# Raw weights of the MLP's second product requested on ScalarE's queue, and the transposes of four tiles put later in TensorE's order

## The chip, the cores and the metric

The kernel runs on one core of a Trainium2 chip. The metric is the device time of one execution in microseconds (us). The median of three runs of the kernel before is 2425.84 us (2425.81 to 2425.9); lower is better.

Engines are named as the profile names them: PE (TensorE, matmuls), DVE (VectorE), ACT (ScalarE), POOL (GpSimd) and SP (SyncE, which in this kernel issues nearly all data transfers). "SPq" in a row of the profile is a transfer being issued from SP's queue.

## The reference

Two layers of a decoder over 1024 positions of width 1024, all float32. In each layer a token mixer (a chunked gated MLP in layer 1, differential attention in layer 2) is followed by the part that the change touches, a dense MLP with a squared ReLU:

```python
def _sqrelu_mlp(x, w_up, w_down):
    return jnp.square(jax.nn.relu(x @ w_up)) @ w_down      # 1024 -> 4096 -> 1024

for i in range(DEPTH):                                     # DEPTH = 2
    h = h + _rmsnorm(mixer(_rmsnorm(h, g_mix_pre[i])), g_mix_post[i])
    f = _sqrelu_mlp(_rmsnorm(h, g_ffn_pre[i]), f_w_up[i], f_w_down[i])
    h = h + _rmsnorm(f, g_ffn_post[i])
    gate = jax.nn.sigmoid(_rmsnorm(h, g_ple_pre[i]) @ ple_w_gate[i] + ple_b_gate[i])
    h = h + _rmsnorm(gate * (p[i] @ ple_w_proj[i]), g_ple_post[i])
```

## The kernel before, in words

**Products of float32.** Every factor is cut in two: a high part that PE takes at full rate (ACT copies it, L516 in the MLP), and the rest (DVE subtracts, L517). A product is then three matmuls (`mm3`, L345, L346, L347), each of 128 by 512 outputs.

**The MLP (`ffn`).** The first product is done in 16 blocks of 256 hidden columns by a scheme of seven products in place of eight; its banks are emptied by DVE (L589) and ACT (L604), squared by ACT (L592, L593), and the hidden values are stored to DRAM (`hid`, L597). The second product runs over `steps`, pairs (g, c): g = 0, 1, 2 with 16 steps c each, and g = 3 with 8. A step is 24 matmuls into the banks of four row tiles p, two halves each. Between two values of g the banks are emptied by `evict(g, p)`: g = 0 by ACT L764 and DVE L765, g = 1 by DVE L767 and L768, g = 2 by DVE L770 to L772.

**What a step needs.** `load_down(n)` requests, seven steps ahead: the raw weights (g = 0 and 1: L708, 512 KB into the first buffer of a pair x, and L709, 256 KB into the second; g = 2: L705, two halves of 256 KB), a combination of weights that an earlier g stored (g = 2: L706), and half of a hidden block (L710, 512 KB, straight into the room where PE reads it). `split_down(n)`, two or three steps ahead, combines the raw weights on DVE (L720 and L721, L725 and L726, L731 and L732), stores a combination for later (L727, L733), and cuts hidden block and weights into one of seven rooms. The first buffers of the pairs come from rings: for g = 1 six (hin, hin, xn, xn, raw, bbc), for g = 2 four (raw, hin, hin, bbc). A buffer is free for the next load when DVE's L517 has cut it.

**The end of g = 2.** For the tiles 0 to 3 the second product is complete there. `whole` finishes the post-norm, loads the residual (L329), adds (DVE L333), stores it, and normalises for the next part: squares on ACT (L321), a root on POOL (L243, L244), a scaled copy on ACT (L323). Then `transpose_to` transposes the tile in two halves on PE (L296, four transposes of 128 by 128 each, into one of two banks `pt` in turn), and each half is cut by ACT (L282) and DVE (L283). The second argument of `whole` says when: `defer` puts the transposes off until PE's order has advanced by that many microseconds of an internal count, 0.417 ns a column (`tick`). `US_F` is 11; so tile p's transposes come 13 + 4p counted us after the place of the call.

**What sets the order.** PE's instructions run in the order in which the code is written. The order on the other engines and queues is made by a scheduler that weighs the whole program, so an edit can move instructions that it does not name. An engine runs its order strictly one after the other; a transfer that is issued on an engine's queue and has to wait makes that engine wait. A transfer also waits until an earlier one that shares its completion counter has landed; the program has eight such counters, which the transfers of SP and ACT take in turn.

Of the kernel before, what the change touches and what calls it, by code (L numbers as in the profile page):

```python
# [43 lines left out]
def f32(ap):  # L44
    return ap.bitcast(F32)


def f32r(ap):
    return ap.bitcast(F32R)
# [82 lines left out]
def _trunk(ctx, tc, nc, a, out):  # L132
# [107 lines left out]
    def rstd_of(ss, n, eps):  # L240

        k = ss.shape[1]
        nc.gpsimd.tensor_scalar(out=ss, in0=ss, scalar1=1.0 / n, scalar2=eps, op0=ALU.mult, op1=ALU.add)  # L243
        nc.gpsimd.tensor_tensor(out=ss, in0=ss, in1=mhalf[:, :k], op=ALU.pow)  # L244
# [7 lines left out]
    US_G, US_P, US_F, US_E, US_L, US_T = 3.0, 10.0, 11.0, 14.0, 11.0, 20.0  # L252
# [73 lines left out]
    def residual(tt, t_ap, rs, hsrc, hdst, pre, gain=None):  # L326

        h = hinR.next()
        nc.sync.dma_start(h, hsrc[tt * P:(tt + 1) * P, :])  # L329
        w = D if pre or tt < NT - 1 else 512  # L330
        for c in range(0, D, w):
            cs = slice(c, c + w)
            nc.vector.scalar_tensor_tensor(out=h[:, cs], in0=t_ap[:, cs], scalar=rs, in1=h[:, cs],  # L333
                                           op0=ALU.mult, op1=ALU.add)
            nc.sync.dma_start(hdst[tt * P:(tt + 1) * P, cs], h[:, cs])
        if pre:
            pre_norm(h, tt, pre, gain)
# [3 lines left out]
    def load_gbc(i):  # L341
        nc.sync.dma_start(gbc, a["g_post"][i:i + 1, :].broadcast_to([P, D]))

    def mm3(ps, lh, ll, rh, rl, start, stop):
        nc.tensor.matmul(ps, lhsT=lh, rhs=rh, start=start, stop=False)  # L345
        nc.tensor.matmul(ps, lhsT=lh, rhs=rl, start=False, stop=False)  # L346
        nc.tensor.matmul(ps, lhsT=ll, rhs=rh, start=False, stop=stop)  # L347
        tick(3 * 512)
# [152 lines left out]
    def resident(i, k):  # L501

        hi, lo = f32r(aux(2 * k)), f32r(aux(2 * k + 1))
        nc.sync.dma_start(f32(lo), pD[i][k])
        split(nc, f32(lo), hi, lo, eng=nc.gpsimd)
        return hi, lo

    def ffn(i, hsrc, hdst, next_weights):
# [10 lines left out]
        down = dn.rearrange("(q r p) (c d) -> q r c p d", r=2, p=P, c=2)  # L519
        down_rows = dn.rearrange("(q r p) d -> q r p d", r=2, p=P)  # L520
# [159 lines left out]
        def cols(x, k):  # L680
            return x[:, k * 512:k * 512 + 512]
# [10 lines left out]
        def load_down(n):  # L692
            g, c = steps[n]
            room = last[c] if g == 3 else rooms[n % 7]
            hi, lo = [f32r(x.rearrange("p k t -> p (k t)")) for x in room]
            wh, hh, wl, hl = hi[:, 0:1024], hi[:, 1024:], lo[:, 0:1024], lo[:, 1024:]
            x = sets[g].next() if g < 3 else None
            if g == 3:
                for k in range(2):
                    nc.sync.dma_start(f32(cols(hl, k)), hid[2 * c + k][:, 3072:])  # L700
                nc.sync.dma_start(f32(wl), t4[c])
            else:
                if g == 2:
                    for k in range(2):
                        nc.sync.dma_start(cols(x[0], k), down[c, k, 1])  # L705
                    nc.sync.dma_start(x[1], cols(t4[c // 2], c % 2))  # L706
                else:
                    nc.sync.dma_start(x[0], down_rows[c, 0])  # L708
                    nc.sync.dma_start(x[1], down[c, 1, 1 - g])  # L709
                nc.sync.dma_start(f32(hl), hid[c][:, g * 1024:g * 1024 + 1024])  # L710
            loaded[n] = wh, wl, hh, hl, x

# [30 lines left out]
        def after(t):  # L743

            for n in range(len(steps)):
                if n - t == lead_s[n]:
                    split_down(n)
            for n in range(len(steps)):
                if n - t == lead_l[n]:
                    load_down(n)  # L750
# [8 lines left out]
        def evict(g, p):  # L759
            m11, m12 = cols(MA[:, p], 0), cols(MA[:, p], 1)  # L760
            m21, m22 = cols(MA[:, p + 4], 0), cols(MA[:, p + 4], 1)
            a_, b_ = PM[p], other[p]
            if g == 0:
                act(m11, a_, AF.Copy)  # L764
                vec(out=m21, in0=b_, in1=m11, op=add)  # L765
            elif g == 1:
                vec(out=m11, in0=a_, in1=m11, op=add)  # L767
                vec(out=m12, in0=b_, in1=m21, op=add)  # L768
            elif g == 2:
                vec(out=m22, in0=a_, in1=m12, op=add)  # L770
                vec(out=m12, in0=b_, in1=m12, op=add)
                vec(out=m21, in0=a_, in1=m21, op=add)  # L772
            else:
                vec(out=m21, in0=a_, in1=m21, op=add)

        def half(tt, cb):
            m = cols(MA[:, tt], cb)
            ssq[tt] = small2[:, tt, :]
            act(xnR.next()[:, 0:512], m, AF.Square, accum_out=ssq[tt][:, cb:cb + 1])
            vec(out=m, in0=m, in1=cols(gbc, cb), op=ALU.mult)  # L780

        def whole(tt, us):
            s = ssq[tt]
            vec(out=s[:, 0:1], in0=s[:, 0:1], in1=s[:, 1:2], op=add)
            rstd_of(s[:, 0:1], D, RMS_EPS)
            residual(tt, MA[:, tt, :], s[:, 0:1], hsrc, hdst, us)

        for m, (g, c) in enumerate(steps):
            wh, wl, hh, hl = cuts.pop(m)
            n_c = NQ if g < 3 else NQ // 2  # L790

            for p in range(4):
                for e in range(2):
                    bank = PM[p] if e == 0 or g == 3 else other[p]
                    cw = slice(e * 512, e * 512 + 512)
                    ch = slice(e * 512 + p * P, e * 512 + p * P + P)
                    mm3(bank, hh[:, ch], hl[:, ch], wh[:, cw], wl[:, cw],
                        c == 0 and (g < 3 or e == 0), c == n_c - 1 and (g < 3 or e == 1))
                if c == n_c - 1:
                    evict(g, p)  # L800
                    if g == 3:
                        half(p + 4, 0)
                        whole(p + 4, US_F + 4.0 * p)
            if g == 1 and c == 4:
                load_gbc(2 + i)
            if g == 2 and 2 <= c < 6:
                half(c - 2, 0)
            if c == n_c - 1 and g == 2:
                for p in range(4):
                    half(p, 1)  # L810
                    whole(p, US_F + 2 + 4.0 * p)
                for p in range(4):
                    half(p + 4, 1)
                next_weights(i)
            after(m)
            if g == 3:
                if c < 4:
                    ws.load()
                elif c < 6:
                    res[i] += [resident(i, 2 * c - 8), resident(i, 2 * c - 7)]  # L820
# [476 lines left out]
    with tc.manual_schedule(engines={mybir.EngineType.PE}):  # L1297
        x = a["x"]
# [30 lines left out]
        def gates(i):  # L1329
# [3 lines left out]
            ws.stop = len(ws.specs)  # L1333

        ffn(0, hD[0], hD[1], gates)
        ple(0, hD[1], hD[2], US_E)
        mixer1(1, hD[2], hD[3])
        ffn(1, hD[3], hD[4], gates)
        ple(1, hD[4], out, 0)

# [72 lines left out]
```

## Time and profile before

| | |
|---|---|
| median of 3 runs | 2425.84 us |
| profiled execution | 2432.34 us, of which the span (first to last instruction) is 2430.6 |
| PE busy | 2338.2 us, 96% of the span |
| DVE, ACT, POOL busy | 1609.4, 1151.7, 235.4 us |
| granted clock of PE, mean | 0.981 of full speed |
| moved by transfers | 441 MB, 181 GB/s on average |

Stages of the MLP in layer 2, by the windows of the trace: g = 0 fills about 1980 to 2058 us (transfer engines busy 0.91 of the time, 324 GB/s, ACT busy for 35.12 of the 78 us), g = 1 about 2062 to 2150 (2058 to 2150: 0.71, 233 GB/s, ACT 31.79 of 92), g = 2 from 2162 to about 2270.

How to read it: PE is busy nearly always, so the time that can be won or lost lies where PE waits, and the list of waits says for whom. A row of the timeline has the start in us, the length, the engine, the line of the kernel, the operation, what it writes and reads with its shape, and in brackets how long the engine stood idle before it and who released it.

### The profile page before, as it was taken

How to read it: one execution, taken by the hardware profiler on the slowest of the kernel's cores; microseconds unless marked ns; L12 is line 12 of the kernel's file. 1: busy time of each engine (PE TensorE's matmuls, PEld its weight loads, DVE VectorE, ACT ScalarE, POOL GpSimd, SP SyncE). 2: the span in 40 equal slices, each digit the busy share in tenths (PEclk: the TensorE clock that was granted, in tenths of full speed). 3: DMA queues.
4: the chain of work that ended last, by engine and by line, in shares of the span. 5: the costliest groups of instructions: out<-in, count | busy, mean ns of one | idle time of the engine just before them, and what ended most of it. 6: DMA issues, size and time to landing. Idle time of an engine off the chain costs nothing. (4 is left out here: it accounts for less than half of the span.)

```text
span 2430.6 us, 30336 instructions
## 1 busy us (share of the span) xinstructions
PE 2338.2 (96%) x10748; PEld 1933.6 (80%) x10748; DVE 1609.4 (66%) x2468; ACT 1151.7 (47%) x1929; POOL 235.4 (10%) x303
## 2 busy tenths in 40 slices
PE   9999999999999899999999989998999999979998
PEld 7888878888778677878887878777888888868787
DVE  4742698777865665563344888778877797565654
ACT  6232555555433345462224766556555554334551
POOL 1100200000000013010001342321000000000310
PEclk9999999999999899999999999999999999989999
DMA  9111445446976765244445765654544598767423
GB/s 335 47 35 53 160 143 189 154 152 216 356 246 222 243 230 174 87 160 151 145 150 184 217 176 143 156 182 136 185 149 164 177 351 275 246 222 246 173 104 121
DMA packets 200424, 441.02 MB, mean 181 GB/s; under 512 B 21040, under 2 KB 55856, under 8 KB 200144
## 3 DMA queue, kind: packets, MB, share of 16 engines
q1 hardware_dynamic: 199840, 437.89, 54.0%
q8 instruction: 85, 1.39, 0.2%
q0 software_dynamic: 432, 1.19, 0.2%
q14 instruction: 67, 0.55, 0.1%
HBM read 310.02 MB, written 133.17 MB: 182 GB/s over the span
## 5 line engine op out<-in xcount | busy, mean ns | idle before, releaser
L357 PE MATMUL pm_a<-w,xh 128*128 128x512 f32 x704 | 223.7, 396 | 1.2 <-ACT w L119 0.9
L357 PEld LDWEIGHTS pm_a<-w,xh 128*128 128x128 f32 x704 | 131.6, 189 | 29.1 <-ACT w L119 2.0
L516 ACT ACTIVATE xh<-xl 128x1024 fp32r<-128x1024 f32 x72 | 75.4, 1055 | 147.4 <-DMA xl<-hid 129.2
L357 PE MATMUL pb<-w,xh 128*128 128x512 f32 x416 | 135.9, 403 | 5.2 <-DVE gbc L950 2.9
L357 PE MATMUL pm_a<-w,xl 128*128 128x512 f32 x352 | 138.6, 394 | 0.0
L516 ACT ACTIVATE w<-ma 128x512 fp32r<-128x512 f32 x134 | 84.1, 631 | 104.6 <-PE pm_a L346 34.9
L517 DVE TENSOR_TENSOR xl<-xl,xh 128x1024 fp32r<-128x1024 f32 x72 | 87.4, 1220 | 50.7 <-ACT xh L516 50.7
L825 POOL DMA_DIRECT2D bbc<-in_ple_b_gate_dram x2 | 1.3, 627 | 1118.4 <-DVE xl L517 1118.4
L345 PE MATMUL pm_a<-xh,w 128*128 128x512 f32 x272 | 106.7, 392 | 0.0
L346 PE MATMUL pm_a<-xl,w 128*128 128x512 f32 x272 | 106.3, 391 | 0.0
L347 PE MATMUL pm_a<-xh,w 128*128 128x512 f32 x272 | 106.3, 391 | 0.0
L516 ACT ACTIVATE s<-s 128x1024 fp32r<-128x1024 f32 x56 | 58.3, 1054 | 92.3 <-DMA s<-hid 84.5
L243 POOL TENSOR_SCALAR small<-small 128x1 f32<-128x1 f32 x104 | 49.4, 475 | 543.0 <-DVE small L390 319.7
L357 PEld LDWEIGHTS pb<-w,xh 128*128 128x128 f32 x416 | 77.5, 191 | 19.6 <-DVE gbc L950 3.1
L517 DVE TENSOR_TENSOR w<-ma,w 128x512 fp32r<-128x512 f32 x134 | 91.2, 683 | 0.0
L517 DVE TENSOR_TENSOR s<-s 128x1024 fp32r<-128x1024 f32 x56 | 67.7, 1221 | 34.4 <-ACT s L516 33.6
L345 PE MATMUL pb<-xh,w 128*128 128x512 f32 x216 | 84.5, 391 | 0.0
L347 PE MATMUL pb<-xh,w 128*128 128x512 f32 x216 | 84.1, 389 | 0.0
L346 PE MATMUL pb<-xl,w 128*128 128x512 f32 x216 | 84.1, 389 | 0.0
L357 PE MATMUL pb<-w,xl 128*128 128x512 f32 x208 | 83.1, 400 | 0.0
L333 DVE SCALAR_TENSOR_TENSOR hin<-ma,small,hin 128x1024 f32<-128x1024 f32 (+1 forms) x49 | 61.6, 1260 | 28.4 <-POOL small L244 13.9
L357 PEld LDWEIGHTS pm_a<-w,xl 128*128 128x128 f32 x352 | 66.6, 189 | 13.0
(468 smaller groups left out, 7005.5 us busy)
## 6 DMA issues: line engine op xcount, KB each, us to landing
xl<-hid SPq DMA_DIRECT2D x56, 512.0 KB, 4.9
ma<-in_f_w_up_dram SPq DMA_DIRECT2D x48, 512.0 KB, 3.6
h<-hin SPq DMA_DIRECT2D x40, 512.0 KB, 3.3
hid<-ma SPq DMA_DIRECT2D x80, 256.0 KB, 2.4
s<-hid SPq DMA_DIRECT2D x40, 512.0 KB, 5.0
hin<-h SPq DMA_DIRECT2D x40, 512.0 KB, 3.4
hid<-xn SPq DMA_DIRECT2D x64, 256.0 KB, 2.8
hid<-hin SPq DMA_DIRECT2D x64, 256.0 KB, 2.8
```

The lines of the kernel that those rows point to most:

```text
L243: nc.gpsimd.tensor_scalar(out=ss, in0=ss, scalar1=1.0 / n, scalar2=eps, op0=ALU.mult, op1=ALU.add)
L333: nc.vector.scalar_tensor_tensor(out=h[:, cs], in0=t_ap[:, cs], scalar=rs, in1=h[:, cs], op0=ALU.mult, op1=ALU.add)
L345: nc.tensor.matmul(ps, lhsT=lh, rhs=rh, start=start, stop=False)
L346: nc.tensor.matmul(ps, lhsT=lh, rhs=rl, start=False, stop=False)
L347: nc.tensor.matmul(ps, lhsT=ll, rhs=rh, start=False, stop=stop)
L357: nc.tensor.matmul(ps, lhsT=xs(l, kc, tt * P), rhs=r[:, cs], start=kc == 0 and k == 0, stop=kc == KC - 1 and k == 2)
L516: act(h, v, AF.Copy)
L517: vec(out=l, in0=v, in1=f32(h), op=sub)
L825: nc.gpsimd.dma_start(bbc, a["ple_b_gate"][i:i + 1, :].broadcast_to([P, D]))
```

## The change

The raw weights of the second product, L705, L708 and L709, are issued on ACT's queue (`nc.scalar`) in place of SP's: 96 transfers per layer. L706 and L710, the stores and everything of g = 3 stay on SP. And the transposes of the tiles 0 to 3 at the end of g = 2 are put off by 5 counted us more.

```diff
             else:
                 if g == 2:
                     for k in range(2):
-                        nc.sync.dma_start(cols(x[0], k), down[c, k, 1])
+                        nc.scalar.dma_start(cols(x[0], k), down[c, k, 1])
                     nc.sync.dma_start(x[1], cols(t4[c // 2], c % 2))
                 else:
-                    nc.sync.dma_start(x[0], down_rows[c, 0])
-                    nc.sync.dma_start(x[1], down[c, 1, 1 - g])
+                    nc.scalar.dma_start(x[0], down_rows[c, 0])
+                    nc.scalar.dma_start(x[1], down[c, 1, 1 - g])
                 nc.sync.dma_start(f32(hl), hid[c][:, g * 1024:g * 1024 + 1024])
...
             if c == n_c - 1 and g == 2:
                 for p in range(4):
                     half(p, 1)
-                    whole(p, US_F + 2 + 4.0 * p)
+                    whole(p, US_F + 7 + 4.0 * p)
```

Both edits move other instructions, in both layers alike but for details. Three places, all of which name tiles as the profile does (`xl`, `s`: rooms of step data; `raw`, `bbc`, `hin_79`, `hin_80`: raw buffers; `t_1_j`: stored combinations of layer 2).

First, the passage from g = 1 to g = 2 in layer 2. SP before, from the store of the second buffer's combination (hid_15 is the hidden block of the last step of g = 1, hid_0 that of the first step of g = 2):

```order
L733 DMA t_1_0_169<-ma 128x512
L706 DMA ma<-t_1_1_170 128x512
L705 DMA hin_80<-in_f_w_down_dram 128x512
L706 DMA ma<-t_1_2_171 128x512
L710 DMA xl_69<-hid_14_159 128x1024
L733 DMA t_1_1_170<-ma 128x512 x2
L706 DMA ma<-t_1_3_172 128x512 x2
L710 DMA xl_70<-hid_15_160 128x1024
L710 DMA s_71<-hid_0_145 128x1024
L705 DMA raw<-in_f_w_down_dram 128x512 x2
L710 DMA xl_70<-hid_1_146 128x1024
```

SP now, from the same store:

```order
L733 DMA t_1_0_169<-ma 128x512
L706 DMA ma<-t_1_2_171 128x512
L733 DMA t_1_1_170<-ma 128x512
L710 DMA xl_69<-hid_14_159 128x1024
L706 DMA ma<-t_1_3_172 128x512
L733 DMA t_1_1_170<-ma 128x512
L706 DMA ma<-t_1_3_172 128x512
L710 DMA xl_70<-hid_15_160 128x1024
L710 DMA s_71<-hid_0_145 128x1024
L710 DMA xl_70<-hid_1_146 128x1024
```

The raw loads are gone, hid_14 stands behind the first of the two stores to t_1_1, hid_15 still behind both, and hid_1 directly behind hid_0. ACT, the same place (steps 32 to 36, + is what is new there):

```order
 L516 ACTIVATE s_71<-raw 128x1024
+L705 DMA raw<-in_f_w_down_dram 128x512
 L516 ACTIVATE s_71<-s_71 128x1024
+L705 DMA raw<-in_f_w_down_dram 128x512
 L516 ACTIVATE xh_68<-hin_79 128x1024
 L516 ACTIVATE xh_68<-xl_70 128x1024
+L705 DMA hin_79<-in_f_w_down_dram 128x512 x2
 L516 ACTIVATE s_73<-hin_80 128x1024
 L516 ACTIVATE s_73<-s_73 128x1024
+L705 DMA hin_80<-in_f_w_down_dram 128x512 x2
 L516 ACTIVATE xh_67<-bbc 128x1024
```

Behind the last row the two halves for bbc stand again with a cut of a hidden half (`xh_67<-xl_69`) between them.

Second, ACT at the end of the first product (layer 1; `gbc` here is a hidden value on its way out, `s_72<-s_72` the cut of a hidden half):

```order
 L516 ACTIVATE xh_68<-ma 128x1024
 L592 ACTIVATE gbc<-gbc 128x512
+L708 DMA raw<-in_f_w_down_dram 128x1024
+L593 ACTIVATE gbc<-gbc 128x512
 L516 ACTIVATE s_72<-s_72 128x1024
-L593 ACTIVATE gbc<-gbc 128x512
 L516 ACTIVATE s_71<-ma 128x1024
+L708 DMA ma<-in_f_w_down_dram 128x1024
+L709 DMA ma<-in_f_w_down_dram 128x512
 L516 ACTIVATE xh_68<-ma 128x1024
```

Raw loads stand among the cuts there, and L593 ahead of a cut that it followed.

Third, the transposes at the end of g = 2 in layer 2. PE now, from the first transposes (24 matmuls later than before) on; the next transposes, of tile 1, come 18 matmuls and one group of transposes behind the first row:

```order
L296 MATMUL pt_88<-identr,ma 128x128 x4
L345 MATMUL pm_c_11160<-xh_68 128x512
L346 MATMUL pm_c_11160<-xl_70,xh_68 128x512
L347 MATMUL pm_c_11160<-xh_68,xl_70 128x512
L296 MATMUL pt_89<-identr,ma 128x128 x4
L345 MATMUL pm_c_11161<-xh_68 128x512
```

ACT at that place, before and now (the two L323 are tiles 0 and 1, the first two L321 tiles 2 and 3):

```order
 L323 ACTIVATE ma<-hin_79,small 128x1024
 L323 ACTIVATE ma<-hin_80,small 128x1024
+L321 ACTIVATE ma,small<-hin_79 128x1024
+L321 ACTIVATE ma,small<-hin_80 128x1024
+L113 ACTIVATE s_72<-s_72 128x1024
 L282 ACTIVATE xh_67<-pt_88 128x4x128
-L282 ACTIVATE xh_67<-pt_89 128x4x128
-L321 ACTIVATE ma,small<-hin_79 128x1024
-L282 ACTIVATE xh_67<-pt_88 128x4x128
-L113 ACTIVATE s_72<-s_72 128x1024
-L321 ACTIVATE ma,small<-hin_80 128x1024
 L323 ACTIVATE ma<-hin_79,small 128x1024
```

L282 of tile 0's first half stood directly behind the two L323; now two L321 and an L113 stand ahead of it.

## The prediction

> **What bounds the kernel now.** I read the page first: TensorE (PE) is busy for 2338.2 of 2430.6 us, so a change can only win or lose time where PE stands still. The list of what each engine waited for, PE's rows, names those places (columns: who waits on whom, us in total, times, longest):
>
> ```profile
> PE pm_c L345 <- DVE ma L767: 12.7, 1, 12.7
> PE pm_a L345 <- DVE ma L767: 9.5, 1, 9.5
> PE pt L296 <- ACT ma L323: 8.8, 2, 4.4
> PE pm_a L345 <- DVE gbc L589: 4.1, 1, 4.1
> PE pb L345 <- DVE ma L765: 3.1, 1, 3.1
> ...
> PE pm_c L345 <- DVE gbc L589: 0.6, 1, 0.6
> ```
>
> The L589 rows are the end of the MLP's first product (layer 1, then layer 2), the others lie in its second. The two L767 waits are one place, once per layer: the passage from g=1 to g=2 (layer 2 has the 12.7). The L323 waits are the first transposes at the end of g=2, once per layer. A stop also costs clock afterwards; the windows around the two places of layer 2, and PE's rows after the long stop, show it:
>
> ```profile
> 2150.00:2180.00 30.00, 16.69 (x57) 13.00 (x57) 24.22 (x31) 13.04 (x18) 0.00 (x0) 0.72 0.66 222
> 2262.00:2300.00 38.00, 33.59 (x153) 27.48 (x152) 22.42 (x28) 24.19 (x39) 16.50 (x14) 0.91 0.64 221
> ```
>
> ```profile
> 2162.75 0.77 PE L345 MATMUL pm_c<-s 128*128 128x512 f32 x1 [12.69 <-DVE ma L767]
> ...
> 2169.43 0.63 PE L346 MATMUL pm_c<-s 128*128 128x512 f32 x1
> 2169.85 0.63 PE L347 MATMUL pm_c<-s 128*128 128x512 f32 x1
> ```
>
> The granted clock is 0.72 and 0.91 there (the number ahead of the last two), and matmuls start 0.42 us apart after the stop, against 0.23 elsewhere (two rows further below). So a stop that vanishes is worth more than its length, but one that only grows costs its growth alone: the slow matmuls behind it are paid already.
>
> **Step one: why PE waits at L767.** Number the steps n = 16g + c, so that 32 is the first of g=2. DVE's rows of layer 2, and SyncE's queue and ScalarE (ACT) beside them:
>
> ```profile
> 2119.84 0.68 DVE L732 TENSOR_TENSOR ma<-ma,hin 128x512 f32<-128x512 f32 x1
> ...
> 2130.77 1.23 DVE L517 TENSOR_TENSOR xl<-xl,xh 128x1024 fp32r<-128x1024 f32 x1 [5.96 <-ACT xh L516]
> 2131.91 1.22 DVE L517 TENSOR_TENSOR s<-raw,s 128x1024 fp32r<-128x1024 f32 x1
> ...
> 2136.71 0.69 DVE L731 TENSOR_TENSOR raw<-raw 128x512 f32<-128x512 f32 x1 [2.44 <-DMA raw<-in_f_w_down_dram]
> ...
> 2144.19 1.22 DVE L517 TENSOR_TENSOR s<-hin,s 128x1024 fp32r<-128x1024 f32 x1
> ...
> 2161.31 0.69 DVE L731 TENSOR_TENSOR raw<-raw 128x512 f32<-128x512 f32 x1 [1.36 <-DMA raw<-in_f_w_down_dram]
> 2161.92 0.68 DVE L767 TENSOR_TENSOR ma<-pm_c,ma 128x512 f32<-128x512 f32 x1
> ```
>
> ```profile
> 2118.07 2.80 SPq L733 DMA_DIRECT2D t<-ma  x2
> 2121.95 1.11 SPq L706 DMA_DIRECT2D ma<-t  x2
> 2123.11 0.42 SPq L710 DMA_DIRECT2D xl<-hid  x1
> ...
> 2133.16 0.81 SPq L705 DMA_DIRECT2D raw<-in_f_w_down_dram  x2
> ...
> 2140.68 0.38 SPq L710 DMA_DIRECT2D s<-hid  x1
> ```
>
> ```profile
> 2129.68 1.06 ACT L516 ACTIVATE xh<-xl 128x1024 fp32r<-128x1024 f32 x1 [6.29 <-DMA xl<-hid]
> ...
> 2145.53 1.06 ACT L516 ACTIVATE s<-s 128x1024 fp32r<-128x1024 f32 x1 [5.33 <-DMA s<-hid]
> ```
>
> The eviction L767 had its input long before (PE stopped at 2162.75 - 12.69 = 2150.06). It stands on DVE behind L731 of step 40, and that L731 ends a loop of five rounds: DVE cuts a raw buffer (L517, over at 2133.13), the buffer is asked for again (L705, 2133.16), lands, is combined (L731, 2136.71), and only then does DVE cut the next buffer. From 2136.71 to 2161.31 it goes round four times, 6.15 us each. The loop's start, 2133.13, hangs on the cut of step 31's hidden half (2130.77, DVE idle for 5.96), on its load's landing (ACT idle for 6.29), and that load was issued at 2123.11, last in SyncE's row behind stores L733 and re-loads L706.
>
> **The change on this place.** In the changed order DVE's rows from L731 of step 36 to L767 are the same but for one swap. A weight load is issued 0.03 us after its buffer comes free now, so SyncE does not hold the loop up and there is nothing for the new queue to shorten. What may shorten is the loop's start. But the order shows step 31's load (hid_15) still behind the same stores L733 and re-loads L706: the last store needs L732 (2119.84), the re-load the end of that store. It therefore goes at about 2123 again; I take no gain. The ends: if it came so early that DVE's 5.96 vanished, -6.0; step 30's load now stands behind a store that it used to precede, and the loads of steps 31 to 33 go out together, so +2.0 (most of the 2.80 us that the two L733 take).
>
> ACT's new order does cost time in the loop, because the raw loads now stand in line with cuts. Steps 36 and 39: the second half's request stands behind the cut of a hidden half, 1.05 us each. Step 38: the pair stands behind the cut at 2145.53, which waits for the load issued at 2140.68 and ends at 2146.59, while DVE frees the buffer at 2144.19 + 1.22 = 2145.41: 1.2 us. Against that the one swap lets DVE cut the bbc buffer ahead of an L732, -0.6. Sum 1.05 + 1.05 + 1.2 - 0.6 = **+2.7 us per layer, +5.4 in all**, with ends of -3.3 and +4.7 per layer. The 96 requests per layer themselves (0.33 us each, as the single SyncE issues) are hidden: ACT is busy for 13.04 of the 30 us of the window above.
>
> A rule speaks against any gain here. The Trainium skill, "DMA: Bandwidth & Descriptors", section "Issuing engines are not separate DMA queues", says that requests from several engines interleave on the same 16 DMA engines, and that a second issuer saves only the sequencer's time of issue. The rows agree as far as they go: the wait is for landing, not for issue. By the rule alone this term would be 0, not +5.4.
>
> **Step two: the start of the second product.** PE's stop at L589 in layer 1:
>
> ```profile
> 608.43 1.06 ACT L516 ACTIVATE s<-s 128x1024 fp32r<-128x1024 f32 x1 [0.74 <-DMA s<-hid]
> 609.40 0.61 ACT L593 ACTIVATE gbc<-gbc 128x512 f32<-128x512 f32 x1
> ```
>
> ```profile
> 609.87 1.22 DVE L517 TENSOR_TENSOR s<-s 128x1024 fp32r<-128x1024 f32 x1
> ...
> 615.68 0.68 DVE L589 TENSOR_TENSOR gbc<-pm_a,hin 128x512 f32<-128x512 f32 x1
> ```
>
> DVE runs without a gap up to this L589, which frees PE's bank. Now ACT has raw loads among its cuts here: a load L708 that must wait for an earlier transfer, the same hidden half that the cut at 608.43 waits for, then L593 (0.61), and only then that cut. So the cut is 0.33 + 0.61 = 0.9 us late. It was ready at 609.49 and DVE took it up at 609.87, so 0.4 of that is hidden and DVE's chain, L589 at its end, is 0.5 late. I take **+0.5 per layer, +1.0 in all**; ends 0 (DVE has other work to put first) and +3 per layer (ACT's next two requests wait for transfers too). In layer 2 the wait is 0.6 today, so nothing hides it there.
>
> The passage g=0 to g=1: in layer 1 the first L765 comes earlier in DVE's order and the last comes behind an L725 that waits for a load. I take 0, and price the bad case as a rival.
>
> **Step three: the transposes.** PE, ACT and DVE rows at the end of g=2, layer 2:
>
> ```profile
> 2269.69 0.39 PE L346 MATMUL pm_c<-s 128*128 128x512 f32 x1
> 2269.92 0.39 PE L347 MATMUL pm_c<-s 128*128 128x512 f32 x1
> 2274.72 1.12 PE L296 MATMUL pt<-identr,ma 128*128 128x128 f32 x4 [4.41 <-ACT ma L323]
> ...
> 2280.33 0.40 PE L345 MATMUL pm_c<-xh 128*128 128x512 f32 x1
> ```
>
> ```profile
> 2273.52 1.15 ACT L323 ACTIVATE ma<-hin,small 128x1024 f32<-128x1024 f32 x1 [4.37 <-POOL small L244]
> ...
> 2280.56 1.06 ACT L321 ACTIVATE ma<-hin 128x1024 f32<-128x1024 f32 x1 [1.95 <-DVE hin L333]
> ...
> 2283.58 1.06 ACT L113 ACTIVATE s<-s 128x1024 fp32r<-128x1024 f32 x1
> ```
>
> ```profile
> 2277.00 0.69 DVE L283 TENSOR_TENSOR xl<-pt,xh 128x512 fp32r<-128x512 f32 x1 [4.72 <-ACT xh L282]
> ...
> 2280.72 1.28 DVE L333 SCALAR_TENSOR_TENSOR hin<-ma,small,hin 128x1024 f32<-128x1024 f32 x1 [0.20 <-DMA hin<-h]
> ```
>
> The first transposes move 24 matmuls down: 24 x 0.23 = 5.5 us, from 2270.15 to 2275.6. L323 ends at 2274.67, so their wait vanishes, with 0.9 us to spare. With the slow work behind it (nine matmuls and two groups of four transposes took 2274.72 to 2280.33, 5.6 us; at 0.23 each, four transposes of 128 columns counted as one matmul of 512, an estimate, they would take 2.5) it is worth 4.4 + 3.1 = 7.5 us per layer.
>
> But ACT's order changes with it. Its cut of tile 0's transposes (L282) stood right behind the two L323; now L321 of tile 2, L321 of tile 3 and L113 stand ahead of it. L321 of tile 3 needs DVE's L333, which starts at 2280.72 on a load of the residual and ends at 2282.00. From there: L321 1.06 and its read 0.18, L113 1.06, L282 0.60, DVE's L283 0.69, about 2285.2 with the small overlaps that such rows have. PE needs the bank back for tile 1's transposes, 18 matmuls and two transpose groups after tile 0's: 2275.6 + 20 x 0.23 = 2280.2. So PE stops there for 5.0 us instead, with the same slow matmuls behind: **+0.6 per layer, +1.2 in all**. The stall goes from L323 to L283; it is not removed. Ends: -7.5 per layer if the cuts come in time, +3 if L333 also comes later by the delays of step one's kind.
>
> **The sum.** 5.4 + 1.0 + 0 + 1.2 = +7.6 us. The profiled execution took 2432.34 us and would take 2439.9; it lies 6.5 us over the median of the runs, so the median goes from 2425.84 to **2433.4**.
>
> **The rivals.**
> - *The transposes' wait really goes* (scheduled rows are late in the order, not in time; ACT is idle for 4.37 ahead of L323, so it has room): -15.0 with the rest as above, 6.4 - 15.0 = -8.6, **2417.2**. Against it: L333 waits for a load that is issued only once L323 frees the buffer.
> - *Both stalls shrink*: with L705 and L709 gone from SyncE, step 31's load no longer comes late, -3.3 per layer, so -6.6 - 15.0 + 1.0 = -20.6, **2405.2**. For it: DVE's 5.96. Against it: the stores L733 stay ahead of that load.
> - *The queue is only a label*: transfers land as before and cuts hide what the order does; only +1.2 is left, **2427.0**. This is what the Trainium skill's rule named above would give.
> - *ACT holds the evictions*: from g=0 to g=1, ACT's L764 and DVE's L765 wait behind a raw load. The price is one landing:
>
> ```profile
> 709.30 0.33 SPq L708 DMA_DIRECT2D bbc<-in_f_w_down_dram  x1
> ```
>
> ```profile
> 714.04 0.69 DVE L725 TENSOR_TENSOR bbc<-bbc 128x512 f32<-128x512 f32 x1 [1.24 <-DMA bbc<-in_f_w_down_dram]
> ```
>
> 4.7 us from issue to use, with L708's issue and L725 5.8, plus 3.1 of slow clock: 8.9 in layer 2, and 8.9 less the 3.1 us of today's wait in layer 1, 14.7 on top of the 7.6, **2448.1**. It decides from the point where that landing comes after the first matmul of g=1 that needs the bank.
>
> **Chances.** The forecast 0.50 (own range 2427 to 2442), the label 0.17, the transposes' gain 0.15, both gains 0.10, the held evictions 0.08. The range 2413 to 2446 leaves out the last two. A measurement of this kernel tells about 0.2%, 4.9 us, from no change; some of the forecast's own range lies within that. Faster 0.25, same 0.20, slower 0.55.
>
> **What would show it.** PE's waits after: L767 at 15.4 (layer 2) and 12.2; no L296 wait on L323, but one of some 5 us per layer on L283; L589 near 4.6 and 1.1. Rounds of L731 between 2133 and 2162 that are 7.2 us long where a cut stands between two L705. I am wrong if step 31's hidden half lands well before DVE's last cut of g=1, if ACT's L282 is ready when PE comes to tile 1, or if PE stops inside g=0.

## The result

The changed kernel takes 2442.76 us (median of 5 runs, 2434.09 to 2443.29), against 2425.9 for the kernel before on the same chip: ratio 1.0055, 95% interval 1.0033 to 1.0076. So it is slower by 16.9 us, with an interval from 8.0 to 18.4. The profiled execution took 2443.29 us with a span of 2441.5. Against the profile shown before it is 10.95 us longer, because that execution lay 6.5 us above its own median. The comparison of places below goes by the two profiles.

PE's waits in the changed kernel (who waits on whom, us in total, times, longest):

```profile
PE pm_c L345 <- DVE ma L767: 17.2, 1, 17.2
PE pm_a L345 <- DVE ma L767: 12.5, 1, 12.5
PE pt L296 <- DVE xl L283: 9.2, 3, 4.6
PE pb L345 <- DVE ma L765: 5.6, 2, 5.2
...
PE pm_a L345 <- DVE gbc L589: 3.5, 1, 3.5
...
PE pm_c L345 <- DVE hin L589: 1.3, 1, 1.3
...
PE pm_a L345 <- DVE hin L589: 1.2, 1, 1.2
...
PE pm_c L345 <- DVE gbc L589: 1.0, 1, 1.0
```

The two long stops at L767 grew from 12.7 to 17.2 us and from 9.5 to 12.5. The stops of the transposes on L323 (8.8 in all) are gone, and stops on L283 stand in their place (4.6 and 4.25; the third, 0.35, lies elsewhere). L765 went from 3.1 to 5.6, L589 has two more rows, on `hin`, and a stop of 0.9 us on ACT's eviction L764 is new. The page's part on DMA queues (packets, bytes, share of the 16 engines' time) shows the move itself:

```profile
q1 hardware_dynamic: 172192, 370.77, 45.1%
q10 hardware_dynamic: 27648, 67.12, 8.4%
```

q10 is ScalarE's queue. The 437.89 MB that were all on q1 before are the same bytes, on two queues.

How much later the changed kernel is, at the first matmul behind a stop (start in us):

| place | before | after | later by |
|---|---|---|---|
| layer 1, behind L589 | 616.50 | 616.47 | 0.0 |
| layer 1, behind L765 | 709.93 | 712.32 | 2.4 |
| layer 1, behind L767 | 807.73 | 813.65 | 5.9 |
| layer 2, behind L589 | 1978.30 | 1984.91 | 6.6 |
| layer 2, behind L767 | 2162.75 | 2176.05 | 13.3 |
| last matmul | 2422.76 | 2433.68 | 10.9 |

Nearly all the loss arises between the end of the first product and L767, in both layers (5.9 and 6.7 us; 0.7 more lies between the two stretches). What comes after L767 in layer 2, the transposes with it, adds nothing; it takes 2.4 us back.

### The profile page after: what moved, and what is told of

Read it like the earlier page. It is cut to its first block, busy times and chain, and to the rows that moved or that the text cites. A ratio compares the mean times of both kernels' runs of the same rounds, so it can differ in the third digit from the quotient of the medians.

```text
span 2441.5 us, 30205 instructions
## 1 busy us (share of the span) xinstructions
PE 2335.0 (96%) x10748; PEld 1929.3 (79%) x10748; DVE 1609.2 (66%) x2468; ACT 1152.0 (47%) x1929; POOL 236.5 (10%) x303
## 4 chain that ended last, share of the span: by engine, by line
PE 69%; DVE 11%; DMA 11%; ACT 4%; issue 3%; POOL 2%; SPq 0%; ACTq 0%; DVEq 0%; POOLq 0%
PE pm_a L357 10%; PE pb L357 6%; PE pm_a L347 5%; PE pm_a L346 5%; PE pm_a L345 5%; PE pb L345 4%; PE pb L346 4%; PE pb L347 4%; PE pm_c L345 4%; PE pm_c L346 4%; PE pm_c L347 4%; PE pm_c L357 3%; DMA xn<-in_f_w_down_dram 1%; DMA raw<-in_f_w_down_dram 1%; DMA t<-ma 1%
## 5 line engine op out<-in xcount | busy, mean ns | idle before, releaser
L516 ACT ACTIVATE xh<-xl 128x1024 fp32r<-128x1024 f32 x72 | 75.4, 1055 | 147.5 <-DMA xl<-hid 82.1
L517 DVE TENSOR_TENSOR xl<-xl,xh 128x1024 fp32r<-128x1024 f32 x72 | 87.4, 1221 | 64.7 <-ACT xh L516 64.6
L516 ACT ACTIVATE w<-ma 128x512 fp32r<-128x512 f32 x134 | 83.8, 630 | 95.7 <-PE pm_a L346 31.4
L516 ACT ACTIVATE s<-s 128x1024 fp32r<-128x1024 f32 x56 | 58.4, 1055 | 103.5 <-DMA s<-hid 48.1
L517 DVE TENSOR_TENSOR w<-ma,w 128x512 fp32r<-128x512 f32 x134 | 91.2, 682 | 0.1
L333 DVE SCALAR_TENSOR_TENSOR hin<-ma,small,hin 128x1024 f32<-128x1024 f32 (+1 forms) x49 | 61.7, 1260 | 42.7 <-DMA hin<-h 27.2
L517 DVE TENSOR_TENSOR s<-s 128x1024 fp32r<-128x1024 f32 x56 | 67.8, 1221 | 32.3 <-ACT s L516 32.2
L357 PEld LDWEIGHTS pm_a<-w,xl 128*128 128x128 f32 x352 | 66.9, 190 | 13.3
```

Source lines behind the costliest of these rows:

```text
L357: nc.tensor.matmul(ps, lhsT=xs(l, kc, tt * P), rhs=r[:, cs], start=kc == 0 and k == 0, stop=kc == KC - 1 and k == 2)
L516: act(h, v, AF.Copy)
L517: vec(out=l, in0=v, in1=f32(h), op=sub)
```

## Experiments

Times are medians; each ratio, with its 95% interval, is to runs of the kernel before on the same chip (medians of 2426.0 to 2427.3 us).

**The two halves of the change.** Alone, the transposes put off by five counted microseconds more:

```diff
-                    whole(p, US_F + 2 + 4.0 * p)
+                    whole(p, US_F + 7 + 4.0 * p)
```

> Only the transposes are put later (by 5 counted us); all raw loads stay on SyncE's queue. My theory: ScalarE's order at the end of g=2 comes from this edit alone, so PE's wait of 4.4 us on L323 turns into one of some 4.6 us per layer on L283 (the changed kernel has 4.59 and 4.25), with the same slow matmuls behind it; L767 stays at 9.5 and 12.7, and the time stays within 3 us of the kernel before. Rival: the order on ScalarE does no harm by itself, both waits vanish, and the time falls by about 15 us to some 2411.

2425.99 us, ratio 0.9997 (0.9981 to 1.0013): no change. And the raw loads alone on ScalarE's queue (the three `nc.scalar` lines of the change):

> Only the queue of the raw loads is changed; the transposes stay where they were. My theory: all of the loss is here, so the time is that of the changed kernel within 3 us (about 11 us over the kernel before, profiled); L767 near 12.5 and 17.2, L765 near 5 in layer 1, L323 back at 4.4 twice and no wait on L283. Rival: the two edits only lose together, and this one alone stays within 3 us of the kernel before.

2437.21 us, ratio 1.0049 (1.0032 to 1.0066). The loss is all in the queue. PE's waits, first of the transposes alone, then of the queue alone:

```profile
PE pm_c L345 <- DVE ma L767: 12.6, 1, 12.6
PE pm_a L345 <- DVE ma L767: 9.8, 1, 9.8
PE pt L296 <- DVE xl L283: 9.3, 3, 4.5
```

```profile
PE pm_c L345 <- DVE ma L767: 15.4, 1, 15.4
PE pm_a L345 <- DVE ma L767: 11.4, 1, 11.4
PE pt L296 <- ACT ma L323: 9.2, 3, 4.4
PE pb L345 <- DVE ma L765: 5.7, 2, 4.9
```

With the transposes alone the wait only changes its name, 8.8 us on L323 to 9.3 on L283 (0.5 of them elsewhere). With the queue alone L767 and L765 grow too, L767 somewhat less than in the whole change. The two halves add up to 10.8 us, inside the interval of the whole change.

**Which loads.** Only the 256 KB halves of g = 2 (L705) moved:

```diff
-                        nc.sync.dma_start(cols(x[0], k), down[c, k, 1])
+                        nc.scalar.dma_start(cols(x[0], k), down[c, k, 1])
```

> Only L705 (the raw halves of g=2) is issued on ScalarE's queue; L708 and L709 stay on SyncE's; transposes as before. My theory: the rounds between step 36's and step 40's L731 are hardly longer (in the changed kernel the second half's request went out as the cut ahead of it started, not when it ended), so L767 grows by about 1 us per layer and the time by 1 to 3 us. Rival, as the prediction had it: the rounds cost 2.7 us per layer, 5.4 in all.

2431.68 us, ratio 1.0028 (1.0014 to 1.0042). Only the loads of g = 0 and 1 (L708, L709) moved:

```diff
-                    nc.sync.dma_start(x[0], down_rows[c, 0])
-                    nc.sync.dma_start(x[1], down[c, 1, 1 - g])
+                    nc.scalar.dma_start(x[0], down_rows[c, 0])
+                    nc.scalar.dma_start(x[1], down[c, 1, 1 - g])
```

> Only L708 and L709 (g=0 and g=1) are issued on ScalarE's queue; L705 stays on SyncE's; transposes as before. My theory: most of the loss is here, 8 to 10 us: L708 into bbc stands behind the eviction L764 that waits for TensorE (2.4 us of load loop lost per layer, felt at L767), and L765 of layer 1 near 5. Rival: if L705 is the cause, the time is within 3 us of the kernel before.

2438.0 us, ratio 1.0054 (1.0039 to 1.007): about all of the loss, though the prediction had put most of it into L705. The profiled execution of this kernel was the shortest of its ten runs (2429.78) and shows no longer L767 (12.0 and 8.9), only L765 of layer 1 at 5.1; that of the kernel with L705 moved (2429.16, also below its median) shows neither (L767 at 11.7 and 9.5, L765 at 2.9). So where these two kernels lose their time the traces don't show. The two losses add up to 17.7 us (12.9 to 27 by their intervals) against 11.0 (7.8 to 16.0) for both moved together; the intervals overlap, so whether they simply add stays open.

**Another engine's queue.** The same three loads with `nc.gpsimd` in place of `nc.scalar`; GpSimd has next to no other work there, so nothing stands ahead of a request:

> The raw loads L705, L708 and L709 are issued on GpSimd's queue, which is nearly idle in these stages, in place of ScalarE's; transposes as before. My theory: the loss comes from raw loads standing in one order with ScalarE's cuts and evictions, not from a second queue, so here L767 and L765 stay near those of the kernel before and the time is within 5 us of it. Rival: two queues whose transfers run at the same time are the cause; then L767 and L765 grow as with ScalarE's queue and the time is 8 us or more over the kernel before. (GpSimd may take longer to issue a transfer, so a loss there alone would not tell the two apart.)

2439.76 us, ratio 1.0059 (1.0039 to 1.0078). The theory that the raw loads lose time behind the cuts in ACT's order had the time near that of before, and finds no support; since GpSimd also takes longer to issue a load (0.54 us against 0.33 for a 256 KB half), this run alone does not refute it. One thing still stood between this and "the queue does it": with each placement the scheduler also puts VectorE's and ScalarE's own instructions into another order.

**Queue and order told apart.** The next three kernels hold VectorE's and ScalarE's computing instructions to a written-out order, by edges that order instructions on one engine and wait for nothing (`_ORDER` lists each engine's instructions). In the traces the rows of VectorE and ScalarE stand in exactly the order of the kernel named, and PE's do too. SyncE's order is not held: of its 1106 other transfers 20 stand in another place than before with the loads on ScalarE's queue, and 132 with the loads on GpSimd's.

```diff
+        _pin(tc, nc, _mybir)
...
+def _pin(tc, nc, mb):
+    traced = {i.name: i for i in nc.cur_bb.bb.instructions}
+    for eng, text in _ORDER.items():
...
+            if prev is not None:
+                tc.add_manual_dep(i, prev.name, mb.DependencyInfo(mb.DependencyClass.NoSync, ...))
+            prev = i
```

Loads on ScalarE's queue, order of the kernel before:

> The raw loads are requested on ScalarE's queue, but VectorE's and ScalarE's computing instructions are held to the order that they have in the kernel before (edges of order alone, no waits). With the raw loads moved, the scheduler had given both engines another order. Theory A, the loss comes from that other order of the cuts and subtractions: within 3 us of before, L767 waits near 11.7 and 9.5 us, L765 near 3. Theory B, the loss comes from the queue itself (requests behind ACTIVATEs in ScalarE's order, transfers of two queues side by side): 8 to 11 us slower, L767 near 15 and 11.5, landings of the 512 KB ma loads 7.3 us against 7.0.

2439.91 us, ratio 1.0049 (1.0029 to 1.0068). Loads on SyncE's queue, order of the kernel with moved loads:

> The other half: every load stays on SyncE's queue, but VectorE's and ScalarE's computing instructions are held to the order that they have when the raw loads are on ScalarE's queue. Theory A (the order): 8 to 11 us slower than before, L767 near 15 and 11.5, L765 near 5 in layer 1, L589 above 3 us and a second stop on hin. Theory B (the queue): within 3 us of before, L767 near 11.7 and 9.5.

2432.44 us, ratio 1.0017 (1.0007 to 1.0028). Loads on GpSimd's queue, order of the kernel before:

> The raw loads on GpSimd's queue, which has next to nothing else to do there, VectorE's and ScalarE's computing instructions held to the order of before. With its own order this queue cost 13.7 us. Theory A (the order): within 3 us of before. Theory B (two queues at once; the landings on this queue were 0.4 to 1.0 us longer): 8 to 14 us slower, L767 near 15 and 11.

2463.98 us, ratio 1.0143 (1.0127 to 1.0159). PE's waits, loads on ScalarE's queue in the order of before, then loads on SyncE's queue in the moved order:

```profile
PE pm_c L345 <- DVE ma L767: 17.4, 1, 17.4
PE pm_a L345 <- DVE ma L767: 15.8, 1, 15.8
...
PE pb L345 <- DVE ma L765: 4.4, 2, 3.3
```

```profile
PE pm_c L345 <- DVE ma L767: 12.1, 1, 12.1
PE pm_a L345 <- DVE ma L767: 9.0, 1, 9.0
...
PE pm_a L345 <- DVE gbc L589: 5.5, 1, 5.5
...
PE pb L345 <- DVE ma L765: 2.8, 1, 2.8
```

With the old order the queue costs its full 12.6 us (7.0 to 16.5; L767 at 17.4 and 15.8). The new order by itself costs 5.2 us (interval 1.7 to 6.8) and lengthens only L589 in its trace (8.2 us in all against 4.7, though the kernel with the transposes alone has the same row of 5.5). So the move to another queue is the cause, with the small changes in SyncE's order that come with it. The scheduler's new order, far from causing the loss, softens it on GpSimd's queue (36.7 us in the old order, 13.7 in the new); on ScalarE's the two can't be told apart (12.6 and 11.0).

The traces side with this at L767: in all five kernels with the three loads moved off SyncE's queue its stops are 14.9 to 18.1 us in layer 2 and 11.0 to 18.6 in layer 1. In the five that leave all of them on SyncE's queue and compute the same product, the kernel before among them, they are 10.9 to 12.7 and 8.7 to 9.8.

**Where the queue loses it.** The rows of the requests at the passage g=0 to g=1 of layer 2, and DVE's row that waits for `bbc`. Before:

```profile
2062.78 0.33 SPq L708 DMA_DIRECT2D bbc<-in_f_w_down_dram  x1
...
2065.86 0.33 SPq L710 DMA_DIRECT2D s<-hid  x1
```

```profile
2067.57 0.69 DVE L725 TENSOR_TENSOR bbc<-bbc 128x512 f32<-128x512 f32 x1 [1.29 <-DMA bbc<-in_f_w_down_dram]
```

The raw load L708 is asked for at 2062.78, the hidden half L710 behind it at 2065.86; `bbc` is used at 2067.57, 4.8 us after its request. Changed kernel:

```profile
2071.40 0.38 SPq L710 DMA_DIRECT2D s<-hid  x1
```

```profile
2071.59 0.33 ACTq L708 DMA_DIRECT2D bbc<-in_f_w_down_dram  x1
```

```profile
2078.80 0.69 DVE L725 TENSOR_TENSOR bbc<-bbc 128x512 f32<-128x512 f32 x1 [2.84 <-DMA bbc<-in_f_w_down_dram]
```

Here the hidden half is asked for 0.19 us *ahead* of the raw load, and `bbc` is used 7.2 us after its request. With both on SyncE, the hidden half stood behind raw loads that wait for their buffers (L708, and at 2065.11 an L705). On a queue without them only a store holds it back (L727, at 2070.98), and its 512 KB are under way together with the load that DVE is waiting for: by the trace the two land at 2078.53 and 2078.71. That they slow each other is a reading of these rows. The DMA engines were not full meanwhile (busy 0.71 of the time from 2071.40 to 2078.70, 251 GB/s), so what exactly slows them stays open. The kernel with loads on ScalarE's queue in the old order has both cases in one execution, first with the raw load ahead, then with the hidden half ahead:

```profile
704.32 0.33 ACTq L708 DMA_DIRECT2D raw<-in_f_w_down_dram  x1
...
2070.62 0.33 ACTq L708 DMA_DIRECT2D bbc<-in_f_w_down_dram  x1
```

```profile
705.33 0.38 SPq L710 DMA_DIRECT2D xl<-hid  x1
...
2070.43 0.38 SPq L710 DMA_DIRECT2D s<-hid  x1
```

```profile
708.51 0.69 DVE L725 TENSOR_TENSOR raw<-raw 128x512 f32<-128x512 f32 x1 [1.49 <-DMA raw<-in_f_w_down_dram]
...
2078.25 0.69 DVE L725 TENSOR_TENSOR bbc<-bbc 128x512 f32<-128x512 f32 x1 [3.56 <-DMA bbc<-in_f_w_down_dram]
```

Raw ahead by 1.0 us: 704.32 to 708.51, 4.2 us. Hidden ahead by 0.19: 2070.62 to 2078.25, 7.6 us. The same count for every L708 on which DVE waited (idle for 0.3 us or more; time from the last request for a buffer of that name to DVE's L725. Three times below 2 us are left out, where that request is already the next one; by the request before it they are 6.8 us in the change, 7.0 with the queue alone and 5.1 with L708 and L709 moved):

| kernel | a hidden half asked for less than 1 us ahead | otherwise: count, range, median |
|---|---|---|
| before | none | 15, 4.4 to 6.05, 5.2 |
| only L705 moved | none | 15, 4.5 to 5.9, 5.1 |
| change | 7.2, 7.3 | 14, 3.9 to 7.05, 5.3 |
| queue alone | 6.9, 7.4 | 14, 3.85 to 7.0, 5.1 |
| only L708, L709 moved | 6.0, 8.4 | 11, 4.2 to 6.0, 4.7 |
| ScalarE's queue, old order | 7.6, 7.7, 7.7, 10.2 | 13, 4.2 to 6.0, 5.0 |

Against the median beside it such a load takes 1.3 to 3.7 us longer, mostly 2 to 2.7, and it happens only where L708 is on the other queue. The 10.2 is not one to compare: it is a load requested early (at 604.38, when the first product of layer 1 still runs), and in the kernel before the load at that place took 7.9 us to land.

On ScalarE's and SyncE's queues it matters how close the two requests are, not only which goes first. The long times among the others (6.8 and 7.05 in the change, 6.5 and 7.0 with the queue alone), and the two of 6.8 and 7.0 left out, belong to loads with a hidden half asked for 0.45 to 0.87 us *behind* them: these six landed after 6.4 to 7.0 us. On one queue, six kernels have eight such loads, with the hidden half 0.42 to 0.95 us behind, and they landed after 5.0 to 5.8 us. (With the raw load on GpSimd's queue a hidden half 0.73 to 0.86 us behind did no harm: 4.8 to 5.5 us.) And a meeting alone does not make L767 longer: the trace with only L708 and L709 moved has two (8.4 and 6.0) and an L767 like that before.

L705 lands later too, where a single half is at stake; before and after, in layer 2:

```profile
2108.49 0.33 SPq L705 DMA_DIRECT2D hin<-in_f_w_down_dram  x1
2108.92 0.38 SPq L710 DMA_DIRECT2D s<-hid  x1
```

```profile
2111.03 0.69 DVE L731 TENSOR_TENSOR hin<-hin 128x512 f32<-128x512 f32 x1 [2.56 <-DMA hin<-in_f_w_down_dram]
```

```profile
2118.37 0.38 SPq L710 DMA_DIRECT2D s<-hid  x1
```

```profile
2119.62 0.34 ACTq L705 DMA_DIRECT2D hin<-in_f_w_down_dram  x1
```

```profile
2124.32 0.69 DVE L731 TENSOR_TENSOR hin<-hin 128x512 f32<-128x512 f32 x1
```

2.5 us from request to use before; 4.7 after, with a hidden half asked for 1.25 us ahead. In this order DVE's cut of the half before it stands in between, but the trace has the load landing at 2124.30, just ahead of its use, so it is the landing that came later.

GpSimd's queue loses in another way as well. Its request and DVE's use, in the loop of rounds before L767, old order:

```profile
2162.07 1.06 POOL L705 DMA_DIRECT2D hin<-in_f_w_down_dram  x2 [6.72 <-DVE xl L517]
```

```profile
2167.09 0.69 DVE L731 TENSOR_TENSOR hin<-hin 128x512 f32<-128x512 f32 x1 [4.18 <-DMA hin<-in_f_w_down_dram]
```

Issuing the pair takes 1.06 us in place of 0.81, and DVE uses it 5.0 us after the request, against 3.55 before (2133.16 to 2136.71), so the rounds of L731 are 7.7 to 10 us long where they were 6.15. Meetings with a hidden half cost less there (four in the old order, 5.5 to 6.3 us against a median of 5.1; one in the new, 8.8, beside three with the hidden half 0.04 to 0.16 us behind, 6.5 to 7.4). How its loss divides between the two I did not settle.

**The order of requests on one queue.** Hidden half first, everything on SyncE:

```diff
+                nc.sync.dma_start(f32(hl), hid[c][:, g * 1024:g * 1024 + 1024])
                 if g == 2:
...
-                nc.sync.dma_start(f32(hl), hid[c][:, g * 1024:g * 1024 + 1024])
```

> One queue as before, and the same order on VectorE, ScalarE, GpSimd and TensorE; only the hidden half of a step is requested ahead of the step's raw weights instead of behind them. It is what a second queue does to the bytes in flight: hidden halves no longer stand behind raw weights. If the bytes' order matters (a part of theory B), the raw weights land later and it is 3 to 6 us slower, with longer L767. If not (theory A), within 2 us of before.

2428.19 us, ratio 0.9998 (0.9985 to 1.0011). This run does not test what it was meant to: SyncE's rows show the scheduler putting the hidden half behind the raw load again (L709 here is the L708 of the other kernels, L703 the hidden half):

```profile
2056.82 0.33 SPq L709 DMA_DIRECT2D bbc<-in_f_w_down_dram  x1
...
2059.88 0.33 SPq L703 DMA_DIRECT2D s<-hid  x1
```

So a run that puts the hidden half ahead on *one* queue is missing. That the meeting of the two transfers lengthens the raw load rests on the table above and on the loads with equal spacing on one and on two queues, not on an edit that makes or breaks it alone. How much of the whole loss these meetings make is not shown.

**The transposes with room.** Tile 0 as in the change, tiles 1 to 3 five counted microseconds later still, loads on SyncE's queue:

```diff
-                    whole(p, US_F + 2 + 4.0 * p)
+                    whole(p, US_F + 7 + 4.0 * p + (5 if p else 0))
```

> As the run with only the transposes put later, but the tiles 1 to 3 come 5 counted us later still (24 matmuls more between tile 0 and tile 1). My theory (the stall is ScalarE's L282 standing behind two L321 and an L113, which are ready at about 2285 where PE comes to tile 1 at 2280): PE now comes at 2285.7, no wait on L323 or L283 of more than 1 us is left, and the time falls by 2 x (4.4 + 3.1) = 15 us to some 2411. Rival: L282 falls behind again by as much as PE is late, a wait of 4 to 5 us stays, and the time is within 3 us of the kernel before.

2422.53 us, ratio 0.998 (0.9969 to 0.9991): faster than both kernels.

```profile
PE pt L296 <- DVE xl L283: 3.3, 3, 1.4
...
PE pm_c L345 <- ACT xh L516: 0.8, 1, 0.8
```

The stop is now mostly gone (3.3 us in all on L283, 8.8 on L323 before), but only about 3 us in layer 2 came of it, not the 7.5 that the prediction gave for its going: from the L772 stop to the last matmul the kernel takes 160.0 us in place of 163.0. The stop of 4.4 us became one of 1.4 on L283 and two small ones on cuts of g = 3 (L516 0.8, L517 0.6), 1.6 us less in all; so some 1.4 us were won on the slow matmuls behind it, to which the prediction gave 3.1.

**Two runs that miss their question.** One raw buffer fewer in g = 2 (three of four), and rooms exchanged at the loop's start, were meant to shift that start:

```diff
-            Ring([(x, cols(MA[:, t], 1)) for t, x in zip(range(4, 8), [raw] + hin + [bbc])]),
+            Ring([(x, cols(MA[:, t], 1)) for t, x in zip(range(4, 7), [raw] + hin)]),
```

> The kernel before with three raw buffers for g=2 in place of four (raw, hin, hin). My theory: PE waits at L767 because VectorE's order puts rounds of the load loop ahead of it, as many as the buffers let the scheduler run ahead; with three buffers one round of 6.15 us fewer stands ahead (eight L731 in place of nine), so L767 falls from 12.7 to about 6.5 and from 9.5 to about 3.4, and the time by 12 us to some 2414. Rival: the wait is a shortage of loaded weights, fewer buffers make it worse, L767 grows by a round (to 19 and 16) and the time rises by 12 us.

2436.47 us, ratio 1.0045 (1.003 to 1.006).

```diff
-            room = last[c] if g == 3 else rooms[n % 7]
+            room = last[c] if g == 3 else rooms[{35: 2, 36: 0, 37: 1}.get(n, n % 7)]
```

> The kernel before, but the steps 35, 36 and 37 take the rooms 2, 0 and 1 in place of 0, 1 and 2, so that step 35's room comes free only when TensorE is done with step 30. My theory: PE waits at L767 because VectorE's order lets five rounds of loads run ahead of it; now the scheduler puts four ahead (eight L731 in all in place of nine), so L767 falls by one round of 6.15 us, to about 6.5 and 3.4, and the time by some 8 to 12 us. Rival: the wait is that much loading and will come back at the next wait behind it (L768 or the data of a later step); then the time is within 3 us of the kernel before.

2431.93 us, ratio 1.0026 (1.0012 to 1.0041). In both, loads run so far ahead that some steps of g = 2 read the raw weights or the hidden half of another step: the work is of the same size, but transfers and cuts depend on each other in another way, so neither says why the loop starts when it does. That stays open. With the rooms exchanged the stops at L767 do go, and stops of 13.8 and 11.0 us on a cut (ACT L516) stand in their place.

## Why the prediction was right, and where it was not

The direction held, and 2442.76 lies inside the range of 2413 to 2446. The size was low: 2433.4 was forecast, 7.6 us above, and 16.9 (8.0 to 18.4) came, more than twice as much and just outside the forecast's own 2427 to 2442. By the profiles 2439.9 was forecast and 2443.29 came, a difference of 10.95 to the profile before. That the total is even this near is partly luck, as the terms show:

**Transposes, +0.6 per layer: right, and by its mechanism.** The stop on L323 vanished and one on L283 of 5.0 us was forecast; it took 4.59 and 4.25, together what L323 had taken (8.8), so the term measured 0. ACT, DVE and PE in layer 2:

```profile
2285.62 1.15 ACT L323 ACTIVATE ma<-hin,small 128x1024 f32<-128x1024 f32 x1 [4.37 <-POOL small L244]
...
2293.77 1.06 ACT L321 ACTIVATE ma<-hin 128x1024 f32<-128x1024 f32 x1 [1.20 <-DVE hin L333]
...
2294.82 1.04 ACT L113 ACTIVATE s<-s 128x1024 fp32r<-128x1024 f32 x1
2295.77 0.57 ACT L282 ACTIVATE xh<-pt 128x512 fp32r<-128x512 f32 x1
```

```profile
2292.45 1.28 DVE L333 SCALAR_TENSOR_TENSOR hin<-ma,small,hin 128x1024 f32<-128x1024 f32 x1 [1.07 <-DMA hin<-h]
...
2296.37 0.69 DVE L283 TENSOR_TENSOR xl<-pt,xh 128x512 fp32r<-128x512 f32 x1 [2.64 <-ACT xh L282]
```

```profile
2297.12 0.91 PE L296 MATMUL pt<-identr,ma 128*128 128x128 f32 x4 [4.25 <-DVE xl L283]
```

L333 of tile 3 waits for its load of the residual and ends at 2293.73, the second L321 follows at 2293.77, then L113, then L282, then L283: the chain that the forecast laid out, one row after the other.

**The passage to g=2, +2.7 per layer: near in size by luck, wrong in its parts.** L767 grew by 3.0 and 4.5 us (12.2 and 15.4 forecast, 12.5 and 17.2 measured). But the step that was to make it, requests behind cuts in ACT's order, is worth at most 0.8 us in layer 2:

```profile
2149.24 0.69 DVE L731 TENSOR_TENSOR raw<-raw 128x512 f32<-128x512 f32 x1 [0.86 <-DMA raw<-in_f_w_down_dram]
...
2174.61 0.69 DVE L731 TENSOR_TENSOR raw<-raw 128x512 f32<-128x512 f32 x1 [2.56 <-DMA raw<-in_f_w_down_dram]
```

From step 36 to step 40 four rounds take 25.37 us where 24.60 stood before, not 27.3. In layer 1 they take 26.3 in place of 25.25, so the rounds make at most 1.9 us of the 7.5 in both layers. The cuts hardly hold a request back:

```profile
2146.06 1.06 ACT L516 ACTIVATE s<-s 128x1024 fp32r<-128x1024 f32 x1 [1.86 <-DVE s L517]
2146.08 0.41 ACTq L705 DMA_DIRECT2D raw<-in_f_w_down_dram  x1
```

The request that stands behind a cut of 1.06 us goes out 0.02 us after that cut *began*, so an engine's strict order does not mean that a request waits for the end of the instruction ahead of it. The prediction charged the whole cut, twice. The loop's start, which it put at 0 with +2.0 as its worst end, came later by more: DVE's use of `bbc` is 11.2 us later than before where PE, behind its stop at L765, is 8.8 later, which makes 2.4; L731 of `hin` adds 2.1, of which 1.0 come back by the next L731 (2118.03 before, 2130.36 after), and the loop starts 3.7 us later by this count (about 2.4 in layer 1). The first is a landing that met a hidden half, the second a landing 1.25 us behind one. The prediction asked whether SyncE was late with raw loads, not what the waiting raw loads kept back behind them.

**The end of the first product, +0.5 per layer: right in layer 1, low in layer 2.** The stops are 4.74 against 4.15 in layer 1 (+0.6) and 2.28 against 0.60 in layer 2 (+1.7). The size in layer 1 is luck again: the first wait fell (3.50 against 4.15), and the second, on `hin`, 1.24 and 1.28 us, was not foreseen. In layer 1 the first matmul behind L589 comes no later than before.

**g=0 to g=1, taken as 0: wrong.** In layer 1 PE's stop at L765 is 5.16 us against 3.10, since the raw load landed 7.3 us after its request in place of 5.3 and DVE's L725 stands ahead of L765; in layer 2 it is 0.43, and the loss goes into the loads ahead of L767 instead. It is the place of the rival on held evictions, at about a third of its price (5.8 forecast in layer 1); the new stop on ACT's L764, 0.91 us in layer 1, belongs to it too, since the cuts and the L764 ahead of that matmul stand behind a request (L708 at 703.04) that waited for its buffer.

The growth of the stops together (7.5 at L767, 2.3 at L589, 2.5 at L765, 0.9 at L764) is 13.2 us; the profiles differ by 10.95 and the medians by 16.9. These differences lie within what single executions of this kernel scatter by (2417.82 to 2433.79 for the kernel before in the last set of runs), and I can't assign them.

**The rivals.** The transposes' wait didn't go, alone or with the queue. The queue wasn't a mere label: moving the loads alone costs 11.0 us. The Trainium skill's rule ("DMA: Bandwidth & Descriptors", section "Issuing engines are not separate DMA queues") says two things: that transfers of several issuers interleave on the same DMA engines, and that a second issuer only saves time of issue, from which no loss follows. The trace agrees with the first as far as it goes: `bbc` and a hidden half, requested 0.19 us apart on two queues, land 0.2 us apart after 7.1 us. On the second it differs: the loss is there, and landings that come later are a part of it.

## What to carry to other kernels

In this kernel a queue that waits was also a gate: what stood behind the waiting request was kept off the DMA engines until the urgent transfer had gone out. Before moving the urgent loads to another queue, look at what they hold back, and at whose transfer then meets them; a landing that is waited for counts, not the time of issue. And a stop that only moves to the next name in the list of waits has a cause further up: shift the work that stands between (here tiles 1 to 3, too), not only the instruction that waits.

## What I had not expected of the hardware

- A DMA request on ScalarE's queue went out just after the start of the ACTIVATE ahead of it, not at its end: 2146.08 behind a cut that runs from 2146.06 for 1.06 us, and likewise 2157.98 behind 2157.85.
- A 512 KB load that was used 5.1 to 5.3 us after its request (median, before and after the change) took 7.2 and 7.3 us when another 512 KB load had been asked for a fifth of a microsecond earlier on another queue. With the other load 0.45 to 0.87 us behind it, it landed after 6.4 to 7.0 us on ScalarE's and SyncE's queues and, with 0.42 to 0.95 us, after 5.0 to 5.8 us on one queue.
- With VectorE and ScalarE held to the same order, the same bytes took 12.6 us more on ScalarE's queue (7.0 to 16.5) and 36.7 us more on GpSimd's (30.8 to 38.6).
